# A fourth up-projection pair by seven half-size products, a last norm on two columns, transfers planned to land later, and modulations and low parts placed anew

## The chip, the cores and the metric

The kernel runs on one NeuronCore of a Trainium2 chip. Its engines work side by side, each through its own list of instructions in order: TensorE (PE in the profile; PEld is its loading of stationary operands), VectorE (DVE), ScalarE (ACT), GpSimd (POOL) and SyncE (SP, which here only issues transfers). They wait for each other by semaphores. The metric is the time of one execution on the device, in microseconds (us).

## What is computed

A trunk of two layers over 512 positions of width 1024 in float32. Layer 0 mixes tokens by retention, layer 1 by an mLSTM; each is followed by a feed-forward part with a causal convolution (3 taps). Every part starts from a normed and modulated copy of the residual stream and is added to it through a gate; shift, scale and gate come from a vector c.

```python
def rmsnorm(x, g):
    xf = x.astype(jnp.float32)
    xn = xf * lax.rsqrt(jnp.mean(xf * xf, axis=-1, keepdims=True) + EPS)
    return xn.astype(x.dtype) * g

def conv_ffn(h, w_up, conv_w, conv_b, w_down):
    u = causal_dwconv(h @ w_up, conv_w, conv_b)
    a, b = jnp.split(u, 2, axis=-1)
    return (jax.nn.silu(a) * b) @ w_down

def reference(x, c, ...):
    c_act = jax.nn.silu(c)
    for i in range(DEPTH):                       # 2 layers
        mod = c_act @ ada_w[i] + ada_b[i]        # 6 * 1024 values
        sh_t, sc_t, gt_t, sh_f, sc_f, gt_f = jnp.split(mod, 6, axis=-1)
        h = rmsnorm(x, norm_tok_g[i]) * (1.0 + sc_t) + sh_t
        y = retention_mixer(h, ...) if i == 0 else mlstm_mixer(h, ...)
        x = x + gt_t * y
        h = rmsnorm(x, norm_ffn_g[i]) * (1.0 + sc_f) + sh_f
        x = x + gt_f * conv_ffn(h, ffn_w_up[i], ffn_conv_w[i], ffn_conv_b[i], ffn_w_down[i])
    return rmsnorm(x, final_g)
```

The feed-forward part has 2816 inner columns, so its up-projection has 22 pairs of 128-column tiles (a and b); tile f and tile f + 22 make pair f.

## The kernel before

**Layout.** Activations are held transposed: eight tiles `x[m]` of 128 channels by 512 positions. "Halves" are positions 0 to 255 (HA) and 256 to 511 (HB).

**Three products for one.** A float32 value v is split into a high part (rounded to TensorE's reduced float32 by a cast on ACT) and a low part, v minus high. A product is then three matmuls: high by high, high by low, low by high (`mm3`, and the loops in `product`). The names in the profile follow from that: `whi` and `wlo` for weights, `hh` and `hl` for the normed input h, `ggh` and `ggl` for the gated inner values, `t24`, `t3` for sums of parts of h.

**Low parts in two ways.** `low_part` subtracts on DVE. `low_part_added` writes the negated high part on ACT (`wlo<-whi`) and lets a transfer issued by POOL add the raw weights to it (the accumulating `wlo<-raw`, `wlo<-wa`, `wlo<-ws`, `wlo<-wt`). Which way each of some 345 low parts takes is a default of its place, turned round for the numbers in the list `SWAPPED`.

**Pairs by seven products.** A tile pair with the whole h can be computed as 2 by 2 blocks (two tiles, two halves of positions; the inner sum in two halves as well) by seven half-size products in place of eight (`Fold`, `folded`, with sums of weight blocks `ws`, `wt`, made on DVE, and sums of h, made once by `Sums`). In each layer's feed-forward part the pairs 0 and 1 are computed while the norm is finished (`pf`), pairs 2 and 3 directly, as 24 products of 512 columns a tile (`pp`, `proj_item`), and pairs 4 to 21 (`FOLD_FROM` = 4) as units of `folded`. A unit is 84 products of 256 columns into two PSUM banks (`p` in the profile; `fs` and `fq` are copies out of them that ACT makes, and which later products into the same place wait for). Beside a unit stand the preparation of the next unit's weights, the convolution and gating of the pair before (`cv`), and, where the inner values are there, two tiles of the down-projection (`po`, with weights `raw` loaded by `Beside` into two buffers that the modulations also use).

**Modulations.** The 96 groups of mod are each a load of 0.5 MB (`ada`) and one multiply-and-sum over 1025 columns on DVE (`gemv`). 16 belong to the start; the other 80 are dealt out to stages by the table `SIDES`.

**The order.** Nothing runs in the order of the code. All calls are recorded (`Plan.add`), and `Plan.order` and `Plan.run` play them through with assumed costs, choosing for every engine the call that is ready and due first; the instructions are then issued in that order. A transfer is assumed to take 2.45 us per MB (5.4 where it accumulates), and what uses it is taken to be ready a fixed time after that: 1.2 us, or 2.4 us for an accumulating one. The due time of a transfer is put ahead of its user's by its length and 3.0 or 4.5 us (`tail`). At run time the real waits are made by semaphores, so a wrong assumption costs waiting in line: an instruction that is ready stands behind one that isn't.

**The start.** `ret_start` norms x by column sums: squares as stationary operand against one column of 1/1024 (`pms<-ones_d,sq`, 128x1), a root and a reciprocal of 4 columns, and a product of each column, repeated, with the identity to spread it over the partitions (`pms<-eye,rc`). Then h is made in eight slices, and the products of slice k wait for `hh` of that slice.

**The end.** The last down-projection is done by halves (`boundary`). `End` norms each half: `SquareSum` adds squares on DVE and splits the sum into two parts, `root` multiplies with a 128x128 matrix of 1/1024 (a mean that stands on all partitions), takes the root on ACT and the reciprocal on DVE over 256 columns; `use` multiplies each tile with gain and reciprocal (`out`) and sends two tiles to HBM at a time.

## Time and profile before

| | before |
|---|---|
| median of 3 runs | 1483.68 us (1481.92 to 1483.88) |
| the profiled execution | 1483.41 us |
| its span, first to last instruction | 1481.6 us |
| mean granted TensorE clock | 0.997 |
| instructions | 27248 |
| HBM read, written | 195.23 MB, 2.12 MB |
| DMA queue q0, POOL's transfers | 116.54 MB, 42.2% of 16 engines' span |
| DMA queue q1, SP's transfers | 197.11 MB, 38.3% |

Times of instructions are microseconds from the span's start. In a timeline a row gives start, duration, engine, line, operation, output <- inputs, shape and count, and in brackets how long the engine stood idle before it and what ended that. All operations are issued through one helper, so every row has the same line (L383), and rows are told apart by the names of tiles. The view of waits has, for an engine, whom it waited for, the total, the number and the longest wait. The view of windows has the busy time of each engine in a stretch. The chain is the work that ended last, followed back through what released it.

### The profile page before, as it was taken

The page shows a single profiled execution, that of the slowest core. Times are in us where ns is not written, and L with a number is a line of the kernel's source. Part 1 is how long each engine was busy: PE and PEld are TensorE (multiplying, and loading weights), DVE is VectorE, ACT ScalarE, POOL GpSimd, SP SyncE. Part 2 cuts the span into 40 slices and gives each one's busy share as a digit, 9 for nine tenths or more (in the row PEclk, how much of TensorE's full clock was granted, in tenths as well). Part 3 has the DMA queues.
Part 4 walks back from the last instruction along what each step waited for, and adds up shares of the span by engine and source line. Part 5 has one row for each costly group of instructions (what it writes and reads, how often), then busy time and mean ns, then how long its engine had stood idle before and what let it go on. Part 6 is the DMA issues. An engine that isn't in the chain of part 4 may idle for free.

```text
span 1481.6 us, 27248 instructions
## 1 busy us (share of the span) xinstructions
PE 1461.3 (99%) x10468; PEld 1368.8 (92%) x10468; DVE 1268.1 (86%) x2136; ACT 1075.9 (73%) x1606; POOL 279.0 (19%) x313
## 2 busy tenths in 40 slices
PE   9999999999999999999999999999999999999997
PEld 6799999998999999999999998999889899999997
DVE  7999979777989889898897999999889887777786
ACT  5678768777577676676668986989856876767662
POOL 0334132322111111111001222132211111111100
PEclk9999999999999999999999999999999999999998
DMA  9868989888798899999457895888687887888751
GB/s 363 252 175 207 282 209 230 224 250 212 206 215 215 241 261 258 265 261 266 118 180 171 207 246 144 208 221 199 205 239 201 213 219 194 194 208 191 190 125 58
DMA packets 93268, 315.65 MB, mean 213 GB/s; under 512 B 12225, under 2 KB 14657, under 8 KB 93138
## 3 DMA queue, kind: packets, MB, share of 16 engines
q0 software_dynamic: 32112, 116.54, 42.2%
q1 hardware_dynamic: 60738, 197.11, 38.3%
q8 instruction: 82, 1.34, 0.4%
q10 hardware_dynamic: 288, 0.27, 0.1%
q14 instruction: 48, 0.39, 0.1%
HBM read 195.23 MB, written 2.12 MB: 133 GB/s over the span
## 4 chain that ended last, share of the span: by engine, by line
PE 86%; DMA 7%; DVE 3%; ACT 2%; issue 2%; POOL 0%; DVEq 0%; ACTq 0%; SPq 0%; POOLq 0%
PE p L383 36%; PE po L383 27%; PE pv L383 9%; PE pav L383 4%; PE pp L383 3%; PE pf L383 3%; DMA wlo<-raw 2%; PE psc L383 2%; DMA raw<-w_in 1%; DMA wb<-w_up 1%; DMA raw<-w_dn 1%; PE pst L383 1%; DMA wlo<-wa 1%; DMA raw<-w_up 1%; PE pms L383 1%
## 5 line engine op out<-in xcount | busy, mean ns | idle before, releaser
L383 PE MATMUL p<-hh,whi 128*128 128x256 f32 (+1 forms) x994 | 275.6, 278 | 1.9 <-DVE p L383 1.9
L383 PE MATMUL p<-hl,whi 128*128 128x256 f32 x992 | 275.1, 277 | 0.0
L383 PE MATMUL p<-hh,wlo 128*128 128x256 f32 x992 | 273.4, 277 | 0.0
L383 ACT ACTIVATE wlo<-whi 128x1024 fp32r<-128x1024 f32 x223 | 235.0, 1057 | 39.8 <-PE po L383 15.1
L383 PEld LDWEIGHTS p<-hh,whi 128*128 128x128 f32 x994 | 187.1, 188 | 2.8 <-DVE p L383 2.3
L383 PEld LDWEIGHTS p<-hl,whi 128*128 128x128 f32 x992 | 186.7, 188 | 0.4
L383 PEld LDWEIGHTS p<-hh,wlo 128*128 128x128 f32 x992 | 185.6, 188 | 0.0
L383 PE MATMUL p<-t24h,whi 128*128 128x256 f32 x744 | 165.0, 279 | 4.1 <-ACT fs L383 3.1
L383 PE MATMUL po<-ggl,whi 128*128 128x512 f32 (+1 forms) x448 | 153.3, 343 | 0.0
L383 PE MATMUL po<-ggh,wlo 128*128 128x512 f32 (+1 forms) x448 | 153.1, 343 | 0.0
L383 PE MATMUL po<-ggh,whi 128*128 128x512 f32 (+1 forms) x448 | 152.4, 343 | 0.0
L383 ACT CAST whi<-raw 128x1024 fp32r<-128x1024 f32 (+1 forms) x117 | 118.0, 1019 | 44.8 <-DMA raw<-w_s 10.5
L383 PE MATMUL p<-t24l,whi 128*128 128x256 f32 x496 | 137.5, 277 | 0.0
L383 DVE SCALAR_TENSOR_TENSOR x<-po,mod,x 128x512 f32<-128x512 f32 (+1 forms) x184 | 113.0, 628 | 23.2 <-PE po L383 22.7
L383 PEld LDWEIGHTS p<-t24h,whi 128*128 128x128 f32 x744 | 126.3, 188 | 6.9 <-ACT fs L383 3.9
L383 DVE SCALAR_TENSOR_TENSOR ada<-ada,c_ext 128x1025 f32<-128x1025 f32 x96 | 119.5, 1246 | 6.5 <-DMA ada<-ada 6.4
L383 POOL DMA_DIRECT2D wlo<-wa x62 | 53.8, 867 | 355.4 <-ACT wlo L383 223.4
L383 PE MATMUL po<-yh,whi 128*128 128x256 f32 (+1 forms) x354 | 116.0, 329 | 0.3 <-ACT o L383 0.3
L383 PE MATMUL po<-yl,whi 128*128 128x256 f32 (+1 forms) x352 | 115.7, 329 | 0.0
L383 PE MATMUL po<-yh,wlo 128*128 128x256 f32 (+1 forms) x352 | 115.6, 329 | 0.0
L383 DVE SCALAR_TENSOR_TENSOR cv<-p,vecs,cv 128x511 f32<-128x511 f32 (+1 forms) x144 | 106.4, 744 | 9.9 <-ACT cv L383 9.2
L383 ACT CAST whi<-ws 128x1024 fp32r<-128x1024 f32 x86 | 90.0, 1050 | 28.5 <-DVE ws L383 23.5
(287 smaller groups left out, 4422.0 us busy)
## 6 DMA issues: line engine op xcount, KB each, us to landing
ada<-ada SPq DMA_DIRECT2D x96, 512.5 KB, 7.4
wlo<-ws POOLq DMA_DIRECT2D x68, 512.0 KB, 6.9
wlo<-wa POOLq DMA_DIRECT2D x62, 512.0 KB, 6.3
wlo<-wt POOLq DMA_DIRECT2D x44, 512.0 KB, 6.9
wlo<-raw POOLq DMA_DIRECT2D x41, 512.0 KB, 8.4
wa<-w_up SPq DMA_DIRECT2D x36, 512.0 KB, 6.9
wb<-w_up SPq DMA_DIRECT2D x36, 512.0 KB, 6.2
raw<-w_o SPq DMA_DIRECT2D x32, 512.0 KB, 6.6
```

What stands on the lines that cost most here:

```text
L383: getattr(c.obj, c.name)(*[real(v) for v in c.a], **{key: real(v) for key, v in c.k.items()})
```

## The change

1. `FOLD_FROM` 4 becomes 3: pair 3 joins the units of `folded` in both layers, so there are 19 units, and pair 2 alone is computed directly. The first down-projections stay beside pair 5 (`LATER`), so two units, pairs 3 and 4, and not one stand ahead of them.
2. `End` norms the last half as the start does: column sums on two columns of 128 positions, root and reciprocal of a 128x2 tile, and spreading by the identity. The gains are multiplied into copies of x on ACT as the tiles come (`xg`), and the last multiplication runs over strips of three, three, one and one tiles, each with its own transfer.
3. The plan's assumptions: loads are ready 2.5 us after their length instead of 1.2, accumulating transfers 3.0 instead of 2.4; loads are due 4.0 us ahead of that length instead of 3.0.
4. `SIDES`, `SWAPPED`, `QLOW` and `ML_LAST` are other numbers: the 80 modulations and the ways of the low parts are dealt out anew (31 instead of 32 modulations beside layer 0's units; the attention of the mLSTM's last head one weight tile later). In all 18 accumulating transfers go and DVE subtracts 20 low parts more.

```diff
-SIDES = [("ret q1", 2), ("ret v1", 2), ("ret g1", 6), ("ret g2", 2), ("ret q3", 2), ("ret g3", 5), ("ret o2", 6), ("fold0", 32), ("end0", 2), ("ml v1", 4), ("ml g1", 1), ("ml q2", 1), ("ml g2", 2), ("ml g3", 2), ("ml o1", 1), ("ml o2", 6), ("up1", 4)]
+SIDES = [("ret q1", 2), ("ret v1", 2), ("ret g1", 8), ("ret v2", 2), ("ret g2", 2), ("ret q3", 2), ("ret g3", 5), ("ret o2", 5), ("fold0", 31), ("end0", 2), ("ml v1", 5), ("ml g1", 2), ("ml q2", 1), ("ml v3", 2), ("ml o1", 6), ("ml o2", 2), ("up1", 1)]
-SWAPPED = (64, 67, 75, 150, 153, 158, 188, 192, 200, 208, 209, 211, 222, 241, 287, 301, 313)
-FOLD_FROM = 4
+SWAPPED = (61, 63, 64, 67, 75, 82, 83, 131, 132, 146, 153, 158, 179, 185, 188, 189, 192, 195, 200, 208, 209, 211, 218, 222, 223, 241, 247, 251, 255, 258, 264, 268, 270, 276, 277, 284, 285, 292, 301, 302, 310, 314, 315)
+FOLD_FROM = 3
+LATER = 5
+LANDING = (2.5, 3.0)
+LEAD = (4.0, 4.5)
-ML_LAST = (0, 1, -1, 2)
+ML_LAST = (1, 2, -1, 2)
-QLOW = (1, 3)
+QLOW = (0, 2)
     def tail(self, c):
-        return c.lat if not c.dma else c.dma + (4.5 if "accum_op" in c.k else 3.0)
+        return c.lat if not c.dma else c.dma + LEAD["accum_op" in c.k]
...
-                c.end = dma_free + (2.4 if "accum_op" in c.k else 1.2)
+                c.end = dma_free + LANDING["accum_op" in c.k]
...
-            if m == KT - self.direct - 1:
+            if m == KT - self.direct - 1 and not self.bare:
                 self.parts = Pair("ss")
                 self.parts.split(self.acc[:, r], r)
...
     class End(Norm):
-        direct = (0, 2)
+        direct, bare = (0, 2), True
+        strips = ((0, 3), (3, 6), (6, 7), (7, 8))
...
+        def square(self, p, m):
+            super().square(p, m)
+            if p:
+                for k0, k1 in self.strips:
+                    if k0 <= m < k1:
+                        if m == k0:
+                            self.scaled[k0] = wide("xg")
+                        at = (m - k0) * 256
+                        A.activation(self.scaled[k0][:, at : at + 256], x[m][:, HB], AF.Copy, scale=self.gain(m))
+
+        def last_root(self):
+            if self.eye is None:
+                self.eye = slot("eye")
+                S.dma_start(self.eye[:, :P], ident)
+            s, ps, out_ps, rc = self.s[1], bank("pms"), bank("pst"), slot("rc")
+            for n, sq in enumerate([s.acc] + s.last):
+                for t in range(2):
+                    PE.matmul(ps[:, t : t + 1], sq[:, 256 + t * P : 384 + t * P], ones["d"][:, :1].bitcast(F32),
+                              start=n + t == 0, stop=True, skip_group_check=True)
+            reciprocal_root(rc, ps[:, :2], slice(0, 2), eps_t[:])
+            for t in range(2):
+                PE.matmul(out_ps[:, 256 + t * P : 384 + t * P], rc[:, t : t + 1].broadcast_to([P, P]),
+                          self.eye[:, :P], start=t == 0, stop=True, skip_group_check=True)
+            self.rs[1] = out_ps
+
+        def last_use(self, k0, k1):
+            n = k1 - k0
+            o, each = wide("out"), lambda t: t.rearrange("p (a t) -> p a t", a=n)
+            V.tensor_tensor(each(o[:, : n * 256]), each(self.scaled[k0][:, : n * 256]),
+                            self.rs[1][:, HB].rearrange("p (a t) -> p a t", a=1).broadcast_to([P, n, 256]), op=ALU.mult)
+            S.dma_start(out[k0:k1, :, HB].rearrange("m p t -> p m t"), each(o[:, : n * 256]))
...
         def rest(self):
-            item([], lambda w: self.root(1))
-            for k in range(0, KT, 2):
-                item([], lambda w, k=k: self.use(1, k, k + 2))
+            item([], lambda w: self.last_root())
+            for k0, k1 in self.strips:
+                item([], lambda w, k0=k0, k1=k1: self.last_use(k0, k1))
...
-            downs = [None] * (5 - FOLD_FROM) + [p for gi in range(len(GROUPS) - 1) for p in self.down(gi)]
+            downs = [None] * (LATER - FOLD_FROM) + [p for gi in range(len(GROUPS) - 1) for p in self.down(gi)]
...
-            self.up(2)
+            th = self.pair(2)
             early(1)
-            th = self.pair(3)
-            proj_item(w[3], self.h, th, True)
+            proj_item(w[2], self.h, th, True)
             early(len(steps))
-            proj_item(w[3 + FT], self.h, lambda ps: (self.start.sums.turn(), th(ps)), True)
+            proj_item(w[2 + FT], self.h, lambda ps: (self.start.sums.turn(), th(ps)), True)
```

What the plan makes of it shows in the order of instructions. Three places follow. On ACT, at the end of layer 0's units, before the change: `whi<-raw` is the cast of the last down-projection weights of 1024 columns, `whi<-ws` and `whi<-wb` are casts of a unit's weights, `fs` is the copy that PE waits for.

```order
L383 CAST ggh_8080<-cv_8001 128x512
L383 CAST whi_8088<-raw_8019 128x1024
L383 CAST whi_8101<-ws_8071 128x1024
L383 CAST whi_8114<-wb_7812 128x512
L383 ACTIVATE cv_8122<-p_1340_7929,vecs 128x512
L383 COPY fs_8130<-p_1365_8104 128x256
```

And the same place after it, on the same engine:

```order
L386 COPY fq_8097<-p_1349_7978 128x256
L386 ACTIVATE cv_8135<-p_1349_7978,vecs 128x512
L386 CAST whi_8146<-ws_8124 128x1024
L386 CAST whi_8158<-wb_7888 128x512
L386 CAST whi_8166<-raw_8101 128x1024
L386 COPY fs_8180<-p_1374_8150 128x256
```

The cast of the loaded weights stood ahead of two casts and the convolution's first step; now it stands behind them, next to the copy `fs`.

On ACT, at the kernel's start, before the change: the four `hh` are the fifth to the eighth slice of h, `whi<-raw` the casts of the last weights of the start's own products and of the first query and key tiles behind them.

```order
L383 ACTIVATE hh_425<-xr_416,mod_86 128x512
L383 CAST whi_430<-raw_356 128x1024
L383 ACTIVATE wlo_440<-whi_430 128x1024
L383 ACTIVATE hh_459<-xr_450,mod_86 128x512
L383 CAST whi_486<-raw_409 128x1024
L383 CAST whi_496<-raw_419 128x1024
L383 ACTIVATE hh_505<-xr_491,mod_86 128x512
L383 ACTIVATE wlo_513<-whi_486 128x1024
L383 ACTIVATE hh_532<-xr_525,mod_86 128x512
```

After it:

```order
L386 ACTIVATE hh_423<-xr_416,mod_86 128x512
L386 CAST whi_428<-raw_348 128x1024
L386 ACTIVATE wlo_442<-whi_428 128x1024
L386 CAST whi_452<-raw_382 128x1024
L386 ACTIVATE hh_461<-xr_454,mod_86 128x512
L386 ACTIVATE wlo_467<-whi_452 128x1024
L386 ACTIVATE hh_503<-xr_496,mod_86 128x512
L386 CAST whi_508<-raw_431 128x1024
L386 CAST whi_516<-raw_439 128x1024
L386 ACTIVATE wlo_526<-whi_508 128x1024
L386 ACTIVATE hh_534<-xr_524,mod_86 128x512
```

One cast has moved ahead of the sixth slice (the second `hh` row), and no cast of a load is left directly ahead of the seventh; two stand ahead of the eighth. The load of that first cast is now issued right behind one modulation row, where two more such rows and another load went first.

On PE, the last rows before the change: `po` is the last down-projection, `pms` the mean of squares.

```order
L383 MATMUL po_17642<-ggh_17333,wlo_17203 128x256
L383 MATMUL pms_17668<-ssh_17638,ones_d 128x256
L383 MATMUL pms_17668<-ssl_17650,ones_d 128x256
L383 MATMUL pms_17668<-sq_17653,ones_d 128x256
L383 MATMUL pms_17668<-sq_17673,ones_d 128x256
```

After it:

```order
L386 MATMUL po_17748<-ggh_17436,wlo_17365 128x256
L386 MATMUL pms_17772<-ones_d,ssq_17598 128x1 x2
L386 MATMUL pms_17772<-ones_d,sq_17757 128x1 x2
L386 MATMUL pms_17772<-ones_d,sq_17776 128x1 x2
L386 MATMUL pst_17787<-eye_17294,rc_17784 128x128 x2
```

Four products of 256 columns have become six of one column, with the sums as the stationary operand, and two of 128 columns that spread the result.

More of the change, by code (lines that the diff above doesn't have):

```diff
@@ L672, in trunk, with __init__ @@
     class SquareSum:
-        def __init__(self, r, direct):
-            self.r, self.acc, self.last, self.direct = r, slot("ssq"), [], direct
+        def __init__(self, r, direct, bare=False):
+            self.r, self.acc, self.last, self.direct, self.bare = r, slot("ssq"), [], direct, bare
         def add(self, m):
@@ L1081, in trunk @@
     class Norm:
-        direct = DIRECT
+        direct, bare, eye = DIRECT, False, None
         def __init__(self):
@@ L1090, in square @@
             if m == 0:
-                self.s[p] = SquareSum(r, self.direct[p])
+                self.s[p] = SquareSum(r, self.direct[p], self.bare and p)
             self.s[p].add(m)
@@ L1214, in trunk, with __init__ @@
     class End(Norm):
-        direct = (0, 2)
+        direct, bare = (0, 2), True
+        strips = ((0, 3), (3, 6), (6, 7), (7, 8))
+        def __init__(self):
+            super().__init__()
+            self.scaled = {}
         def gain(self, m):
             return col("final", m)
+        def square(self, p, m):
[27 more added lines that the diff above has]
+            S.dma_start(out[k0:k1, :, HB].rearrange("m p t -> p m t"), each(o[:, : n * 256]))
         def use(self, p, k0, k1):
```

## The prediction

> **What bounds the kernel now.** First the page, for the shares; then the chain of waits; then PE's own waits.
>
> ```profile
> PE 1461.3 (99%) x10468; PEld 1368.8 (92%) x10468; DVE 1268.1 (86%) x2136; ACT 1075.9 (73%) x1606; POOL 279.0 (19%) x313
> ```
>
> TensorE is busy for 99% of the span, so time comes out in two ways alone: fewer matrix products, or shorter stretches in which PE waits. The next rows are all the long waits that the view of waits has for PE (us in total, times, longest).
>
> ```profile
> PE p L383 <- ACT fs L383: 3.1, 4, 1.3
> PE p L383 <- DVE p L383: 2.9, 4, 1.3
> PE pst L383 <- ACT hh L383: 1.6, 2, 1.0
> ```
>
> Together 7.6 us; the rest of what the span has beyond PE's busy time lies at the start and behind the last product. What a product costs must not be read from its duration. Two rows of the groups by shape (busy us, mean ns of one), then two pieces of the chain (start, us, what, count):
>
> ```profile
> L383 PE MATMUL p<-hh,whi 128*128 128x256 f32 x992 | 275.5, 278 | 1.9 <-DVE p L383 1.9
> ...
> L383 PE MATMUL pp<-hh,whi 128*128 128x512 f32 x104 | 40.5, 389 | 0.0
> ```
> ```profile
> 66.21 21.76 PE pp L383 x96
> ...
> 485.33 8.17 PE p L383 x72
> ```
>
> The means, 278 and 389 ns, overlap their neighbours. In the chain 96 products of 512 columns take 21.76 us, 226.7 ns each, and 72 of 256 columns 8.17 us, 113.5 ns each. Half the width is half the price, with nothing fixed on top.
>
> **Part 1, the pair by seven products.** Per layer 48 products of 512 columns go and 84 of 256 come; in both layers 96 and 168. 96 x 226.7 ns is the 21.76 us of the row above; 168 x 113.5 ns is 19.07 us. **Minus 2.7 us.** Around it DVE gets the sums of the folded weights. What that meets is read from the windows (us, then PE, PEld, DVE, ACT, POOL busy, clock, DMA share, GB/s):
>
> ```profile
> 425.00:441.00 16.00, 16.00 (x73) 13.25 (x72) 9.66 (x16) 13.78 (x18) 3.45 (x4) 1.00 0.93 209
> 470.00:485.00 15.00, 15.00 (x110) 14.01 (x109) 13.26 (x23) 9.72 (x15) 1.72 (x2) 1.00 1.04 288
> 485.00:650.00 165.00, 165.00 (x1188) 154.13 (x1187) 146.77 (x252) 114.74 (x159) 24.19 (x28) 1.00 0.94 254
> 800.00:900.00 100.00, 98.82 (x780) 96.00 (x779) 93.18 (x152) 88.44 (x141) 24.28 (x30) 1.00 0.88 224
> ```
> ```profile
> 485.37 0.75 DVE L383 SCALAR_TENSOR_TENSOR x<-po,mod,x 128x512 f32<-128x512 f32 x1
> ```
>
> A unit of the fold with down-projections (470 to 485) has 13.26 us of DVE work beside 15 us of PE. The change gives each layer one more unit without them: without two residual adds of 0.75 us DVE keeps 11.8 us, PE only 84 x 113.5 ns = 9.5 us. DVE is 2.3 us short in that unit, at most 4.6 us in the two layers. I cost it at nothing: just ahead of it, from 425 to 441, DVE is idle for 6.3 of 16 us, and in the long run of units (485 to 650) PE still never waits. Once that idle time is spent, the 2.3 us per layer show.
>
> **Part 2, the last half norm.** The end before, by engine: DVE, ACT, PE, and the chain's last piece of products.
>
> ```profile
> 1470.78 0.49 DVE L383 SCALAR_TENSOR_TENSOR x<-po,mod,x 128x256 f32<-128x256 f32 x1 [0.91 <-PE po L383]
> 1473.01 1.75 DVE L383 RECIPROCAL rs<-rs 128x256 f32<-128x256 f32 x1 [1.75 <-ACT rs L383]
> 1474.80 3.26 DVE L383 SCALAR_TENSOR_TENSOR out<-x,vecs,rs 128x256 f32<-128x256 f32 x8
> ```
> ```profile
> 1471.30 0.42 ACT L383 ACTIVATE sq<-x 128x256 f32<-128x256 f32 x1 [1.71 <-DVE x L383]
> 1472.51 0.47 ACT L383 ACTIVATE rs<-pms,eps_t 128x256 f32<-128x256 f32 x1 [0.79 <-PE pms L383]
> ```
> ```profile
> 1471.77 0.70 PE L383 MATMUL pms<-sq,ones_d 128*128 128x256 f32 x2 [0.35 <-ACT sq L383]
> ```
> ```profile
> 1458.02 12.74 PE po L383 x108
> ```
>
> Residual, square, mean, root, reciprocal, eight multiplications; DVE ends at 1478.06. The same form of sum on columns, root, reciprocal and spreading by the identity stands at this kernel's start; the last row is the nearest to a wide multiplication.
>
> ```profile
> 13.10 3.57 PE pms L383 x16
> 17.31 2.09 PE pms L383 x8
> ```
> ```profile
> 16.78 0.27 ACT L383 ACTIVATE rc<-pms,eps_t 128x4 f32<-128x4 f32 x1 [0.85 <-PE pms L383]
> ```
> ```profile
> 17.08 0.18 DVE L383 RECIPROCAL rc<-rc 128x4 f32<-128x4 f32 x1 [2.03 <-ACT rc L383]
> ```
> ```profile
> 1431.69 0.95 DVE L383 TENSOR_TENSOR wlo<-raw,whi 128x768 fp32r<-128x768 f32 x1
> ```
>
> Sixteen records for eight one-column sums: 0.223 us a record, two records a sum. The change has six sums after PE's last product, 12 records, 2.68 us from 1470.76, to 1473.44 (the last square is ready at 1471.72 and finds four sums still running). Root 0.27 and reciprocal 0.18, each with 0.04 to start: 1473.97. Two spreading products, half of the eight records in 2.09 us: 1475.02, and 0.05 to start. Then two multiplications of 768 columns at 0.95 and two of 256 at 0.41 (3.26 over eight): 2.72, to 1477.8. **Minus 0.3 us.** Bounds: minus 1.1, if four of the sums vanish under the residual and square, and plus 0.5, if the last transfers wait for each other. The eight scaled copies on ACT cost nothing: ACT stands idle 1.71 us before each square, and the last copy (0.42, after the square) ends before PE is done.
>
> The Trainium skill, "TensorE: Matmul & The Clock Gate", section Back-to-back issue gap, gives about 60 cycles (25 ns) to products of 1 to 64 columns. By it the twelve records would take 0.3 us as an estimate and the sum of all parts would come out some 1.5 us lower. This trace has 223 ns a record, nine times that, so the measurement decides.
>
> **Part 3, transfers planned to land later.** No instruction is added; the plan assumes that loads land 1.3 us later (accumulating ones 0.6), and puts other work ahead of what uses them. In the old plan a 512 KB load on a free queue lands 0.4 + 1.2 + 1.33 + 1.2 = 4.1 us after its issue starts, in the new one at 5.4. The trace:
>
> ```profile
> raw<-w_dn SPq DMA_DIRECT2D x32, 512.0 KB, 7.6
> ```
>
> So the old plan was too early, the new one less so. Two of PE's waits come from that. At the end of layer 0's fold:
>
> ```profile
> PE p L383 <- ACT fs L383: 1.3, 1, 1.3
> ```
> ```profile
> 681.41 0.60 ACT L383 CAST ggh<-cv 128x512 fp32r<-128x512 f32 x1
> 685.41 1.05 ACT L383 CAST whi<-raw 128x1024 fp32r<-128x1024 f32 x1 [3.39 <-DMA raw<-w_dn]
> 686.37 1.05 ACT L383 CAST whi<-ws 128x1024 fp32r<-128x1024 f32 x1
> 687.32 0.61 ACT L383 CAST whi<-wb 128x512 fp32r<-128x512 f32 x1
> 687.83 0.78 ACT L383 ACTIVATE cv<-p,vecs 128x512 f32<-128x512 f32 x1
> 688.50 0.36 ACT L383 COPY fs<-p 128x256 f32<-128x256 f32 x1
> ```
>
> ACT stands 3.39 us at a cast whose load is late; behind it queue two casts, a convolution and the copy fs that PE needs. In the new order those three come first and the cast stands directly ahead of fs (the order's rows, above): with the load at the same moment fs starts some 2.1 us earlier (688.50 less 686.37), more than PE's 1.3 us. **Minus 1.3.** At the start:
>
> ```profile
> PE pst L383 <- ACT hh L383: 1.0, 1, 1.0
> ```
> ```profile
> 53.27 1.05 ACT L383 CAST whi<-raw 128x1024 fp32r<-128x1024 f32 x1 [1.42 <-DMA raw<-w_in]
> 54.23 0.72 ACT L383 ACTIVATE hh<-xr,mod 128x512 fp32r<-128x512 f32 x1
> ```
> ```profile
> ada<-ada SPq DMA_DIRECT2D x1, 512.5 KB, 7.6
> ```
>
> The seventh slice of h stands behind that cast. In the new order one load goes out right after the modulation row issued at 35.58 (the last row above, landed 7.6 us later, at 43.2); its cast moves ahead of the sixth slice. An estimate: 0.5 MB more at about 340 GB/s is 1.5 us, so it lands at 44.7, and cast and slice end near 46.5; PE wants the sixth slice 24 x 226.7 ns = 5.4 us before its wait at 53.65, at 48.2. Nothing new is late, and PE's 1.0 us goes. **Minus 1.0.** For the other 5.3 of the 7.6 us I take no change: their places are reordered too, and the rows say neither way. Bounds for this part: minus 7.6, if all go, and plus 2.3, if two waits as long as these two come new.
>
> **Part 4, modulations and low parts placed anew.** 80 gemvs stay 80. 18 accumulating transfers go; DVE has 20 low parts more, ACT 18 negations fewer.
>
> ```profile
> 873.75 1.22 DVE L383 TENSOR_TENSOR wlo<-ws,whi 128x1024 fp32r<-128x1024 f32 x1
> ```
>
> 20 x 1.22 is 24 us of DVE over 1480, about five a stage. In the stage with least room (800 to 900) DVE is busy 93.18 of 100 us: 6.8 us of room against 4 x 1.22 = 4.9. Cost nothing, up to 4.9 us without that room.
>
> **The sum**, made against the profiled execution's own 1483.41 us (span 1481.6 and 1.8 around it; the median of the runs, 1483.68, is 0.02% above): 1483.4 - 2.7 - 0.3 - 1.3 - 1.0 = **1478.1 us**.
>
> **Rivals.**
> - The waits only move: landings change in the plan, but loads still go out when a buffer comes free, and the two late heads turn up elsewhere. For it: DMA share 0.93 to 1.04 in the windows. Against: the casts have demonstrably changed places with fs. Time: 1483.4 - 3.0 = 1480.4, on either side of it by one wait.
> - More waits go: the remaining 5.3 us as well, since the plan is nearer to the landings everywhere. For it: the other eight are waits for ACT or DVE too. Against: no row above shows a late load ahead of them. Time: 1478.1 - 5.3 = 1472.8.
> - DVE becomes the bound (the slower side). Place: the unit without down-projections in both layers, and the mLSTM's stage around 800 to 900. Price 4.6 + 4.9, and the two late heads stay: 1483.4 - 3.0 + 9.5 = 1489.9. It decides once DVE's idle time ahead of the unit falls under 2.3 us, or the room in the stage under 4.9; with about half of it the time is unchanged. For it: 93%. Against: 6.3 us idle before the fold.
> - Narrow products pay a fixed cost: if 278 and 389 ns were prices, a pair would cost 84 x 0.278 - 48 x 0.389 = 4.7 us more, and the sum would be 1483.4 + 9.4 - 2.6 = 1490.2. The pieces of the chain (113.5 against 226.7 ns) leave it next to nothing. The Trainium skill, "Perfetto Trace Analysis", section Matmuls, does say that larger matmuls are more efficient where possible; in this trace 256 columns are as efficient as 512.
>
> **Chances.** Forecast 0.48; waits only move 0.28 (0.10 of it faster, 0.18 the same); more waits go 0.08; DVE 0.15 (0.11 slower, 0.04 the same); fixed cost 0.01, slower. Faster by over 0.2% 0.66, within 0.2% 0.22, slower by over 0.2% 0.12; 0.2% (3 us) is about what a measurement of this kernel can tell from no change. The forecast's own range is 1475.5 to 1480.4. The range for 8 in 10 goes from 1474.0, most of the way to where all waits go, to 1486.5, about half way into DVE's case.
>
> **What would show it.** 1: the groups have 72 pp products of each kind instead of 104, and x84 pieces where x72 stood in the extra unit. 2: PE's one-column records end near 1473.4 less what was saved ahead, the reciprocal is under 0.2 us, DVE ends 2.7 us behind the spreading. 3: no row of PE waiting for fs near the fold's end or for hh near 53 us. 4: DVE's share about 88%. Wrong if PE waits for DVE p or fs in the fold's first units, or if the waits' sum stays above 6 us.

## The result, and the profile after

| | before | after |
|---|---|---|
| median | 1482.80 us (1480.26 to 1484.13, 21 runs) | 1485.12 us (1483.02 to 1489.25, 21 runs) |
| ratio to before, 95% interval | | 1.0017 [1.0011, 1.0024] |
| the profiled execution | 1483.41 us | 1483.02 us |
| its span | 1481.6 us | 1481.2 us |

The changed kernel is 2.3 us slower, within the 0.2% that the prediction called no change, and not 5.3 us faster as forecast. The two profiled executions hide this: that of before lies 0.6 us above its median, that of after is the shortest of its 21. What the trace shows of after is its best case. The experiments below hold a second execution of each order: up to the tail, run alone2 issues the instructions of before and run undo2 those of after.

First the answers to the rows shown of before: from the page, and from the groups by shape.

```profile
PE 1460.8 (99%) x10550; PEld 1372.3 (93%) x10550; DVE 1292.4 (87%) x2167; ACT 1064.9 (72%) x1604; POOL 267.1 (18%) x295
```
```profile
L386 PE MATMUL pp<-hh,whi 128*128 128x512 f32 x72 | 28.0, 390 | 0.0
```

72 direct products of each kind instead of 104, and a DVE share of 87%: the change did what it said. The view of waits for PE (us in total, times, longest):

```profile
PE p L386 <- DVE p L386: 4.8, 6, 1.6
...
PE pv L386 <- ACT fs L386: 1.4, 1, 1.4
PE pst L386 <- ACT hh L386: 1.3, 1, 1.3
...
PE p L386 <- ACT fs L386: 1.1, 1, 1.1
```

Together 8.6 us, where there were 7.6 before; the one for `hh` is now the first slice of h at 20 us, not the seventh at 53. The prediction said that more than 6 us would prove it wrong. (The sum moves between executions: in alone2, with the order of before, the same three rows give 5.4 us.) To see where the time went, PE's timeline is read at places that both programs have: the first product behind the start (`pp`), of layer 0's feed-forward part (`pf`), of layer 1's values (`pv`), of layer 1's feed-forward part, and the last of the down-projection. Before, then after:

```profile
66.05 0.39 PE L383 MATMUL pp<-hh,whi 128*128 128x512 f32 x1
...
402.14 0.28 PE L383 MATMUL pf<-hh,whi 128*128 128x256 f32 x1
...
771.19 0.39 PE L383 MATMUL pv<-whi,hh 128*128 128x512 f32 x1
...
1131.29 0.28 PE L383 MATMUL pf<-hh,whi 128*128 128x256 f32 x1
...
1470.46 0.28 PE L383 MATMUL po<-ggh,wlo 128*128 128x256 f32 x1
```
```profile
66.38 0.39 PE L386 MATMUL pp<-hh,whi 128*128 128x512 f32 x1
...
406.32 0.28 PE L386 MATMUL pf<-hh,whi 128*128 128x256 f32 x1
...
775.43 0.39 PE L386 MATMUL pv<-whi,hh 128*128 128x512 f32 x1
...
1133.91 0.28 PE L386 MATMUL pf<-hh,whi 128*128 128x256 f32 x1
...
1471.65 0.28 PE L386 MATMUL po<-ggh,wlo 128*128 128x256 f32 x1
```

| stage | before | after | change |
|---|---|---|---|
| start | 66.05 | 66.38 | +0.33 |
| retention | 336.09 | 339.94 | +3.85 |
| layer 0's feed-forward part | 369.05 | 369.11 | +0.06 |
| mLSTM | 360.10 | 358.48 | -1.62 |
| layer 1's feed-forward part | 339.17 | 337.74 | -1.43 |
| tail, to the end of the span | 11.14 | 9.55 | -1.59 |

Half of the 2.7 us of products shows in full, in layer 1 (-1.43). The half of layer 0 is gone, the tail gives five times what was forecast, and retention, where PE has the same products as before, takes 3.9 us more. In the mLSTM three waits of before, at 802, 878 and 1047 us (0.8, 0.7 and 1.5 us), are gone; the longest one there is now 0.45.

The second executions, alone2 and undo2, say which of these changes are firm. From alone2 to undo2 retention takes 3.9 us more as well (336.98 and 340.86), the mLSTM 2.2 less (360.62 and 358.45), layer 1's feed-forward part 1.6 less (338.90 and 337.30). But layer 0's feed-forward part takes 367.41 and 371.63, which is 4.2 us more, where the table has 0.06: from execution to execution of one order it moves by 1.6 to 2.5 us. The table's best case of after therefore hides a loss there.

What PE loses at one place is given below from start to start of two products, less the 113.5 or 226.7 ns that the first one takes; the view of waits counts 0.1 to 0.3 us less.

**Retention.** DVE, then POOL, at the longest new wait, PE's 1.77 us from 214.19 on:

```profile
211.85 3.82 DVE L386 TENSOR_TENSOR wlo<-wv,whi 128x1024 fp32r<-128x1024 f32 x1 [0.77 <-ACT whi L386]
215.60 0.42 DVE L386 TENSOR_TENSOR p<-p,fs 128x256 f32<-128x256 f32 x1
```
```profile
210.79 1.62 POOL L386 TENSOR_TENSOR rp<-rp,rp 128x512 f32<-128x512 f32 x1
212.04 1.21 POOL L386 DMA_DIRECT2D wlo<-ws  x1
212.66 1.92 POOL L386 TENSOR_TENSOR rp<-rp,rp 128x512 f32<-128x512 f32 x1
```

The low part `wlo` takes 1.21 us elsewhere and 3.82 here: 2.61 more. The two additions of POOL beside it cover 0.56 and 1.92 us of the row, 2.48 together. The short sum `p` that PE waits for stands behind it, though its other input was there at 212.1 (`fs`, 211.71 and 0.37 us on ACT). At 122 us PE waits 1.57 us for a copy `fs` in the same way. A sum on DVE took 4.19 us beside two additions of POOL, ACT stood 3.90 us for it, and caught up with its casts ahead of `fs`. The row of DVE, then ACT's:

```profile
111.62 4.19 DVE L386 TENSOR_TENSOR ws<-ws,wv 128x1024 f32<-128x1024 f32 x1
```
```profile
115.85 1.06 ACT L386 CAST whi<-ws 128x1024 fp32r<-128x1024 f32 x1 [3.90 <-DVE ws L386]
...
120.32 1.04 ACT L386 CAST whi<-ws 128x1024 fp32r<-128x1024 f32 x1
121.26 0.61 ACT L386 CAST qkh<-rp 128x512 fp32r<-128x512 f32 x1
121.78 1.05 ACT L386 ACTIVATE wlo<-whi 128x1024 fp32r<-128x1024 f32 x1
122.74 0.56 ACT L386 COPY z<-pav 128x512 f32<-128x512 f32 x1
123.20 0.37 ACT L386 COPY fs<-pv 128x256 f32<-128x256 f32 x1
```

Such long rows are in both traces: those over 0.15 us above the median of their tiles and shape exceed it by 26.5 us in all before and 24.6 after. What differs is who stands behind them. The Trainium skill, "SBUF — State Buffer", section SBUF: two separate sides, says that VectorE and GpSimd share a pair of ports which one of them, the one that starts first, holds for a whole instruction while the other is blocked. The 2.48 and 2.61 us agree with the blocking. Who comes first does not agree: the row of 4.19 us began at 111.62 and POOL's two additions at 111.87 by the profile, and still DVE's row is the long one (spans on POOL are rough).

**The folds' first units.** DVE, then ACT, at layer 0's first wait (444.17, 1.35 us): the sum `p` stands behind two steps of a convolution.

```profile
443.71 1.53 DVE L386 SCALAR_TENSOR_TENSOR cv<-pf,vecs,cv 128x511 f32<-128x511 f32 x2
445.16 0.42 DVE L386 TENSOR_TENSOR p<-p,fs 128x256 f32<-128x256 f32 x1
```
```profile
444.59 0.37 ACT L386 COPY fs<-p 128x256 f32<-128x256 f32 x1
```

The convolution holds the sum up by 0.2 us only, since its input `fs` ends at 444.96. The other 1.15 us are the way from PE's product over the copy and the sum back to PE. At layer 1's wait (1171.77, 1.22 us) the sum does stand in line, behind two sums of weights (0.68 us each).

**The tail**, on PE, then the chain's pieces for root, reciprocal, spreading and the first strip:

```profile
1471.77 0.50 PE L386 MATMUL pms<-ones_d,ssq 128*128 128x1 f32 x4
1472.14 0.58 PE L386 MATMUL pms<-ones_d,sq 128*128 128x1 f32 x4
1472.96 0.61 PE L386 MATMUL pms<-ones_d,sq 128*128 128x1 f32 x4 [0.24 <-ACT sq L386]
```
```profile
1473.61 0.27 ACT rc L386
...
1473.90 0.18 DVE rc L386
...
1474.12 0.72 PE pst L386 x4
...
1474.87 0.95 DVE out L386
```

Four one-column records take 0.37 us up to the next row (inside a row they start 0.11 us apart), and not 0.223 each, which the prediction took from the kernel's start. So the sums have caught up and wait 0.24 us for the last square.

### The profile page after: what moved, and what is told of

Same layout as the page of the kernel before. It is cut to its first block, busy times and chain, and to the rows that moved or that the text cites. A ratio compares the mean times of both kernels' runs of the same rounds, so it can differ in the third digit from the quotient of the medians.

```text
span 1481.2 us, 27389 instructions
## 1 busy us (share of the span) xinstructions
PE 1460.8 (99%) x10550; PEld 1372.3 (93%) x10550; DVE 1292.4 (87%) x2167; ACT 1064.9 (72%) x1604; POOL 267.1 (18%) x295
## 5 line engine op out<-in xcount | busy, mean ns | idle before, releaser
L386 PE MATMUL p<-hh,whi 128*128 128x256 f32 x1026 | 284.3, 278 | 2.5 <-DVE p L386 2.5
L386 PE MATMUL p<-hl,whi 128*128 128x256 f32 x1024 | 283.5, 277 | 0.0
L386 PE MATMUL p<-hh,wlo 128*128 128x256 f32 x1024 | 281.2, 277 | 0.0
L386 ACT ACTIVATE wlo<-whi 128x1024 fp32r<-128x1024 f32 (+1 forms) x205 | 215.4, 1055 | 26.3 <-PE po L386 15.6
L386 PEld LDWEIGHTS p<-hh,whi 128*128 128x128 f32 x1026 | 193.0, 188 | 3.7 <-DVE p L386 3.1
L386 PEld LDWEIGHTS p<-hl,whi 128*128 128x128 f32 x1024 | 192.8, 188 | 0.5
L386 PEld LDWEIGHTS p<-hh,wlo 128*128 128x128 f32 x1024 | 191.3, 188 | 0.0
L386 PE MATMUL p<-t24h,whi 128*128 128x256 f32 x768 | 170.1, 278 | 3.3 <-DVE p L386 2.2
L386 DVE SCALAR_TENSOR_TENSOR x<-po,mod,x 128x512 f32<-128x512 f32 (+1 forms) x184 | 113.5, 628 | 30.6 <-PE po L386 29.8
L386 DVE SCALAR_TENSOR_TENSOR cv<-p,vecs,cv 128x511 f32<-128x511 f32 (+1 forms) x152 | 111.2, 743 | 12.5 <-ACT cv L386 12.2
L386 POOL DMA_DIRECT2D wlo<-wa x55 | 47.6, 866 | 353.6 <-ACT wlo L386 168.7
```

What stands on the lines that cost most here:

```text
L386: getattr(c.obj, c.name)(*[real(v) for v in c.a], **{key: real(v) for key, v in c.k.items()})
```

## The experiments

Theories. **A**: each part saves what it should, and new waits take it back. **B**: what is missing is room on DVE (and on the queues), so whatever is late is late again. **C**: it is the order; PE's short operations stand in line behind work that could wait, and lists such as `SWAPPED` fit the one order for which they were made. Three more are set against C on the way: **D**, the new waits belong to the parts one by one; **E**, 2.5 us is a bad value for the landing; **L**, late loads. Each ratio below is to the kernel before as it ran beside that run (medians 1482.58 to 1483.07 us). The changed kernel did not run again; comparisons with its 1485.12 go across sessions, so its ratio of 1.0017 [1.0011, 1.0024] is the one to compare with.

| run | median us | ratio to before, 95% |
|---|---|---|
| alone1 | 1487.91 | 1.0035 [1.0022, 1.0048] |
| alone2 | 1481.37 | 0.9990 [0.9977, 1.0002] |
| alone3 | 1489.14 | 1.0043 [1.0030, 1.0056] |
| alone4 | 1489.26 | 1.0050 [1.0031, 1.0068] |
| undo1 | 1486.23 | 1.0021 [1.0012, 1.0030] |
| undo2 | 1485.98 | 1.0019 [1.0011, 1.0028] |
| undo3 | 1489.60 | 1.0043 [1.0027, 1.0059] |
| undo4 | 1492.73 | 1.0066 [1.0053, 1.0079] |
| jitter_b | 1488.69 | 1.0035 [1.0023, 1.0047] |
| jitter_a | 1491.21 | 1.0050 [1.0034, 1.0066] |
| moved | 1482.54 | 0.9994 [0.9983, 1.0004] |
| pool_adds | 1497.39 | 1.0094 [1.0079, 1.0108] |
| moved2 | 1481.18 | 0.9987 [0.9976, 0.9998] |
| best_b | 1482.20 | 0.9994 [0.9985, 1.0002] |

### One part alone, on the kernel before

```diff
# alone1
-FOLD_FROM = 4
+FOLD_FROM = 3
+LATER = 5
...
# alone2: End, SquareSum and Norm as changed
# alone3: LANDING and LEAD as changed
# alone4: SIDES, SWAPPED, ML_LAST and QLOW as changed
```

> The kernel before with part 1 alone (pair 3 by seven half-size products in both layers). Theory A, the parts save what they should and new waits from the new order take it back: 2.7 us of products go, new waits of about 1.2 us stand in the first units of both folds (as at 444 and 1171 us in the changed kernel) in place of the 0.9 us that stand there before, so about 1 us faster than before. Theory B, DVE's added work is itself the cost: a unit without down-projections is 2.3 us short of DVE in each layer, waits of 4.6 us, so 2 us slower than before. The prediction on record: 2.7 us faster.

> The kernel before with part 2 alone (last half norm on two columns). Theory A: as in the trace of the changed kernel, where the span ends 9.55 us after the last down-projection product starts and not 11.1, 1.6 us faster than before. The prediction on record: 0.3 us faster. Theory B has nothing to say here.

> The kernel before with part 3 alone (transfers planned to land later). Theory A: the waits at 53 us (1.1) and 687 us (1.4) go, but the whole order is made anew, and new waits of the kind seen at 121 and 214 us of the changed kernel (4 us in retention) come in their place: 1 to 3 us slower than before. Theory B: no instruction is added, so the same as before. The prediction on record: 2.3 us faster.

> The kernel before with part 4 alone (modulations and low parts dealt out anew; the list of turned low parts counts through the program, and with pair 3 direct its entries behind layer 0's first units fall on other low parts than in the changed kernel). Theory A: no work is added on PE, waits move, between 1 us faster and 3 us slower, and where it is slower the waits stand in retention. Theory B: 20 more low parts on DVE cost up to 5 us where DVE has least room (800 to 960 us), about 3 us slower, with PE waiting for DVE there. The prediction on record: no change.

Part 2 alone gives 1.7 us less in the median, as A expected from the trace, though its interval just reaches 1. Each of the other parts alone makes the kernel 5 to 6 us slower, which is more than A, B or the prediction had, while all four together cost 2.3 us: the parts do not add up. Their traces show the waits in line. In alone1 DVE stands 5.42 us for a load, and PE loses 2.7 us behind it, in layer 0's first units (and as much again in layer 1's, at 1207 us, where ACT stands 5.75 us for a load):

```profile
491.98 0.69 DVE L384 TENSOR_TENSOR ws<-wb 128x512 f32<-128x512 f32 x1 [5.42 <-DMA wb<-w_up]
```

In alone4, DVE and then ACT: DVE waits for the load of a modulation; `qkl`, 1.49 us for two, stands behind it, `fs` waits for `qkl`, and PE 4.6 us for `fs`.

```profile
317.00 1.23 DVE L383 SCALAR_TENSOR_TENSOR ada<-ada,c_ext 128x1025 f32<-128x1025 f32 x1 [4.30 <-DMA ada<-ada]
...
319.82 1.49 DVE L383 TENSOR_TENSOR qkl<-rp,qkh 128x512 fp32r<-128x512 f32 x2
```
```profile
321.42 0.37 ACT L383 COPY fs<-p 128x256 f32<-128x256 f32 x1 [4.72 <-DVE qkl L383]
```

Behind this wait TensorE runs at half its clock for 5 us. The window of alone4 right after it (clock in the third column from the end):

```profile
322.00:327.00 5.00, 5.00 (x24) 5.00 (x25) 2.63 (x4) 3.85 (x5) 0.00 (x0) 0.50 1.02 386
```

Products of 256 columns start 0.21 us apart there, not 0.11, which costs 2.5 us more. Wait and slow stretch together are 7.3 us, where before loses 1.2 at the same place: that is about all that alone4 loses. The same happens in undo3 (4.3 us at 316 us, then 2.5), and after alone1's wait at 1207 us (2.7 us, then 1.7), but not after its wait of 2.7 us at 492. So one long wait of PE can be most of what a new order costs. B's place for part 4, 800 to 960 us, is not where alone4 loses its time.

### One part undone, on the changed kernel

```diff
# undo1
-FOLD_FROM = 3
-LATER = 5
+FOLD_FROM = 4
...
# undo2: End, SquareSum and Norm as before
# undo3
-LANDING = (2.5, 3.0)
-LEAD = (4.0, 4.5)
+LANDING = (1.2, 2.4)
+LEAD = (3.0, 4.5)
# undo4: SIDES, SWAPPED, ML_LAST and QLOW as before
```

> The changed kernel with part 1 undone (pair 3 computed directly again, tail, landings and tables as changed; the low parts behind layer 0's units are counted differently, so some entries of the list fall on others). Theory C, every part that makes the plan anew costs about 5 to 6 us by waits elsewhere, as parts 1, 3 and 4 did alone, and the parts fit each other in the changed kernel: slower than the changed kernel, by the 2.7 us of products and some waits, about 1488 us. Theory D, the waits belong to the parts one by one, and part 1's are those in the first units of the folds (444 and 1171 us, 2.6 us together): these go, the products' 2.7 us come back, and the time stays at about 1485.

> The changed kernel with part 2 undone (last half norm as before). Both theories: the tail's 1.6 us come back, 1486.7 us, since nothing ahead of the last products is ordered otherwise.

> The changed kernel with part 3 undone (landings 1.2 and 2.4 us, lead 3.0 as before). Theory D: the wait of 1.6 us at 122 us and the 0.4 us behind it, which the kernel with part 3 alone has too, belong to part 3 and go; about 1483 us. Theory C: tables and landings fit each other, new waits come elsewhere, 1487 to 1491 us.

> The changed kernel with part 4 undone (modulations and low parts dealt out as before). Theory B, 20 more low parts on DVE cost time: up to 3 us faster than the changed kernel, 1482 to 1485 us. Theory C: 1487 to 1491 us, with the longest waits where loads land late, since 18 more accumulating transfers share the queues.

Parts 3 and 4 are harmful alone, and yet without them the changed kernel is slower, by 4.5 and 7.6 us (medians; C had at most 6 for undo4). That is again what a new order costs, and no measure of what a part is worth. B's forecast for part 4, up to 3 us faster without it, fails; a small cost of its 20 low parts could still hide under the new order. D's wait at 122 us does go in undo3, and others take its place (4.3 us at 316 us is the longest), as C expected. undo1, at 1486.23, lies between what C (1488) and D (1485) said. undo2 loses 0.9 us in the median; its interval overlaps that of the changed kernel, so the tail's gain is shown by alone2 and the traces rather than by it.

Two more things follow. In undo1, the view of waits has no row at all from 440 to 505 us and from 1150 to 1225: the waits in the folds' first units are part 1's. Layer 0's feed-forward part, measured as above, takes 367.1 us in it against 369.1 in the changed kernel (371.6 in undo2), though it has 1.36 us more of products, and layer 1's takes 337.69 against 337.74: what the products save there goes into waits as well. What undo1 loses it loses in the mLSTM (364.0 us against 358.5), where part 1 changes no product. And undo2 runs the changed kernel's order up to the tail: a second execution of it. There PE waits 4.4 us in layer 0's first units (440 to 505 us), where the first execution had 1.8, because loads land later. The first of them shows in a cast on ACT, in undo2 and in the changed kernel:

```profile
462.80 1.05 ACT L386 CAST whi<-wa 128x1024 fp32r<-128x1024 f32 x1 [2.56 <-DMA wa<-w_up]
```
```profile
460.00 1.04 ACT L386 CAST whi<-wa 128x1024 fp32r<-128x1024 f32 x1
```

The first execution got the load in time (4.9 us after its issue), the second did not (9.2 us). A second load, for the cast of `raw` at 500 us, landed 9.6 us after its issue where the first execution had 8.4. That fits a median of the changed kernel above its trace, as far as two executions can tell.

### A tenth of a microsecond

```diff
# jitter_b, on the kernel before
-                c.end = dma_free + (2.4 if "accum_op" in c.k else 1.2)
+                c.end = dma_free + (2.4 if "accum_op" in c.k else 1.3)
# jitter_a, on the changed kernel
-LANDING = (2.5, 3.0)
+LANDING = (2.6, 3.0)
```

> The kernel before with one assumption of the plan changed by 0.1 us: loads are taken to land 1.3 us after their length, not 1.2 (the changed kernel has 2.5). Some 440 of DVE's 2041 instructions and 350 of ACT's 1591 come in another place. Theory C (the tables fit the one order they were made with, and any new order meets some waits): 3 to 6 us slower than before, as with the landing of 2.5 us alone. Theory E (the landing of 2.5 us is too late as a value, and that cost the 6 us of part 3 alone): a twelfth of the step, so within 1 us of before.

> The changed kernel with the landing of loads assumed at 2.6 us, not 2.5. Theory C: 2 to 6 us slower than the changed kernel, 1487 to 1491 us. Theory E: within 1 us of it, 1484 to 1486 us.

Both are 6 us slower (1488.69 against 1482.58, 1491.21 against 1485.12). As a value, 2.5 us can hardly be worse than 1.2 when 1.3 costs the same 6 us: E falls. Of the eight runs whose order is made anew, for whatever reason, seven are 4.5 to 7.6 us slower than the kernel that they start from; undo1, at 1.1 us, is the exception. Why the two kernels' own orders are the good ones is argued and not shown: lists that fit one order, as C says, and an order that was merely picked out of many as the fastest would look the same, and no run fits the lists anew.

### The waits moved away by hand

```diff
-        for n in self.order():
+        for n in moved(self, self.order()):
...
+MOVED = ((869, 957), (943, 957), (695, 957), (895, 970), (882, 970), (698, 983), (856, 996),
+         (1869, 1821), (4122, 4254), (4121, 4254), (11914, 11809), (11805, 11809))
```

A pair (n, m) sets call n directly behind call m on its engine; all else keeps its order and its buffers, so nothing is planned anew.

> The changed kernel with twelve instructions set behind another one of their own engine, in five places, and nothing else: on ACT three ahead of the copy fs that PE waits for at 122 us and two ahead of the next one; on DVE two modulations behind the sums pv at 126 us, the low part of 3.82 us behind the sum p at 214 us, two steps of a convolution behind the sum p at 444 us, and two weight sums behind the sum p at 1171 us. Theory C (waits in line: PE's short operations stand behind long ones that could wait): the five waits, 1.57, 0.38, 1.77, 1.35 and 1.22 us, go and little comes instead: about 6 us faster than the changed kernel, 1478 to 1480 us, faster than before. Theory B (DVE has no room there, so whatever is put back is late next): most of it returns within the next units, 1483 us or more.

2.6 us come back, and 6 had been expected. Its trace has 0.42 us of the 1.57 at 122 us and nothing of the waits at 126 and 214: C holds in retention (337.5 us instead of 339.9). In layer 0's first units PE still waits, at 446, 464, 472 and 496 us, 5 us in all. That looks like B, but the moves did not bring the last three: undo2, in which nothing was moved, has them at the same products (467, 475 and 500 us) and as long (3.9 us in all in either run). Of the wait at 444 us only the 0.2 us behind the convolution could go; 1.2 us stay. The rest of that question is moved2's.

### POOL's additions against DVE

```diff
             getattr(c.obj, c.name)(...)
+            if n in EXTRA:
+                c.obj.tensor_tensor(self.spare[:], self.spare[:], self.spare[:], op=ALU.add)
```

> The changed kernel with 28 additions of 128x512 on POOL more, on a tile that nothing else uses, one behind each of POOL's transfers beside layer 0's units from 500 to 690 us; the order is otherwise the same. If DVE stands still while POOL adds (as the rows suggest in which DVE took 3.82 us for 1.21 beside two such additions): each takes up to 1.3 us from DVE, which has 20 us of room in these 190, some 25 us in all, so PE waits 5 us or more in this stretch, and rows of DVE there show up to 1.3 us above their usual length. If DVE and POOL run beside each other and the long rows had another cause: no change, 1484 to 1486 us.

12 us more, and DVE's rows exceed the median of their tiles and shape by 51.9 us in all, not 24.6: the 28 additions took 27.3, near the 25 that were forecast. Windows (us, then PE, PEld, DVE, ACT, POOL busy) of the changed kernel and of pool_adds:

```profile
500.00:690.00 190.00, 189.71 (x1352) 176.32 (x1351) 169.66 (x286) 128.13 (x178) 24.19 (x28) 1.00 0.91 247
```
```profile
500.00:690.00 190.00, 182.97 (x1279) 168.31 (x1280) 182.07 (x265) 121.68 (x170) 53.85 (x54) 0.99 0.86 232
```

DVE does 21 instructions fewer in the same 190 us and is busy 12.4 us longer, while ACT's mean row stays at 0.72 us. That DVE stands still beside POOL's additions is shown; and the stretch loses 6.7 us of PE although DVE still has 8 us idle: the blocked rows need not fill DVE to hold PE up.

### The rest, and the old order mended

```diff
# moved2: moved, and
+         (4453, 4451), (4642, 4470), (4706, 4642), (4643, 4706),
# best_b: alone2, and
+MOVED = ((411, 305), (412, 308), (6614, 6661), (6616, 6633), (6615, 6633), (8009, 7840), (8010, 7840),
+         (8495, 8755), (8612, 8754), (10383, 10541), (10493, 10541), (10668, 10541))
```

> The kernel with five places moved (1482.5 us), and two more beside layer 0's first units: on SP the load of down-projection weights (raw, used 18 us later) goes out behind the two loads of the unit's own weights, not ahead of them; on DVE a modulation, whose buffer the next raw load waits for, comes 2.4 us earlier, ahead of two steps of a convolution. Theory L (the waits at 464 and 496 us, 1.3 and 2.0 us, come from loads that go out late behind a full queue or a held buffer): both shrink by 1 us or more, about 1480 us. Theory B (in the units without down-projections something is always late, since nothing lies beside the chain of copy and sum): they move on to the next instruction, 1482 to 1483 us. The wait of 1.2 us at 446 us stays in both: there PE waits for its own last sum by way of the copy fq and the sum p, with no other product to do.

> The kernel before with part 2 alone (1481.4 us) and eleven instructions set behind another one of their own engine, in five places: the cast at 54 us behind the slice hh, the cast of late raw weights at 685 us behind two casts and a convolution step, two weight sums behind the sum p at 801 us, a modulation and an exponential behind fs and p at 877 us, and a low part and two sums behind the sum p at 1045 us. Theory C (waits in line): 0.8, 0.3 to 1.4, 0.9, 0.7 and 1.3 us go, 4 to 5 us in all, 1477 to 1478 us: faster than both kernels by over 0.2%. Theory B: less than half of it, 1479.5 us or more.

moved2 is faster than both kernels, by 1.8 us against before; its interval ends just below 1 (0.9998). In its profiled execution, the third fastest of 12, the waits at 464 and 496 us are gone, as theory L had it: they were late loads, one behind a load that was needed 18 us later, one for a buffer that a modulation held. That they are gone would prove little alone, since the first execution of the changed kernel did not have them either. But the load of `raw` was as slow as in moved (9.7 us from issue to landing against 10.1) and still landed at 491.57, ahead of its cast at 491.69, because it went out sooner. The 1.2 us at 446 us stay. PE's last product ahead of it, the copy `fq` (ACT), the sum (DVE) and PE again:

```profile
445.47 0.28 PE L386 MATMUL p<-hh,whi 128*128 128x256 f32 x1
446.75 0.38 PE L386 MATMUL p<-t24h,whi 128*128 128x256 f32 x1 [1.00 <-DVE p L386]
```
```profile
445.86 0.36 ACT L386 COPY fq<-p 128x256 f32<-128x256 f32 x1
```
```profile
446.27 0.42 DVE L386 TENSOR_TENSOR p<-p,fq 128x256 f32<-128x256 f32 x1
```

With down-projections in the unit there is a piece like this one of the changed kernel's chain to put between; a unit without them has nothing:

```profile
1223.94 2.75 PE po L386 x12
```

That is what part 1 pays in layer 0 for its 1.36 us.

best_b (twelve moves, where its expectation counts eleven) is a miss: 1482.20, no better than alone2. Its profiled execution reaches the last down-projection product 3.0 us sooner than before (1467.5 against 1470.5), and four of the five waits are gone or smaller, but the one at 877 us grew from 0.7 to 1.6 us: the exponential that was set behind one `fs` now brings its table load (1.28 us) ahead of the next. This execution is the fastest of its 12 (1479.0 to 1484.4), and one of the five waits was no lasting one: at 687 us alone2, with the order of before, loses 0.3 us and not 1.4. Which waits make the median was not seen.

## Why the prediction was wrong

- **Part 1, products: right** (-2.7; -1.43 in layer 1, and the piece of 84 products is there, at 1426.33). **Its cover: wrong.** "I cost it at nothing" took DVE's 6.3 us of idle time ahead of the unit for the cover. DVE still had 4.0 us of it (12.05 busy of the same 16 us in the changed kernel), but the unit has no products to lay beside the chain of copy and sum (1.2 us) and the loads behind it came late (1.3 and 2.0 us more in some executions). The rival named the place and the sign (PE waits for DVE `p` in the fold's first units), with want of DVE as the cause, which was at most a part of it. Against before, layer 1 took 1.4 us less, and layer 0 none less in the one pair of executions and 4.2 more in the other. Against undo1, which has the other new parts without this one, layer 1 gained 0.4 us at most and layer 0 nothing.
- **Part 2: the mechanism right, the size off** by the term of the sums: 12 records at 0.223 us, where they took 0.11. The 0.223 came from a row of the start in which TensorE ran slow (last section). From the last down-projection product to the end of the sums 1.9 us passed, not 3.0, and the spreading took 0.7, not 1.05. Measured -1.6, beyond the bound of -1.1. The reciprocal (0.18 against 0.18) and DVE's end behind the spreading (2.5 against 2.7) were as forecast. The 25 ns that the prediction took from the Trainium skill, "TensorE: Matmul & The Clock Gate", section Back-to-back issue gap, would have been too little by four times; the section itself calls its table the gap of an isolated product, without the loading of the stationary operand, and here every record loads its own.
- **Part 3: the step that failed.** The two waits that it was to remove did go: no wait for `hh` near 53 us, none for `fs` near 687. The second was partly luck, since alone2, with the order of before, has only 0.3 of its 1.4 us. But "for the other 5.3 of the 7.6 us I take no change" treated a plan that is made anew as if it stayed where no row was looked at. Waits went there too (three in the mLSTM), and longer ones came: 3.9 us in retention. The bound "plus 2.3, if two waits as long as these two come new" was the right thought at half its size or less: part 3 alone made the kernel 6.1 us slower, 5.0 of it in retention (341.09 us against 336.09). That an assumption nearer to the real landings gives a better order does not hold here with the lists kept: alone3 and jitter_b are both nearer, and both 6 us slower. The term for a new order was missing from parts 1 and 4 as well.
- **Part 4, no change: cannot be told from the rest.** Alone it makes the kernel 6 us slower, and undoing it does so by 7.6, both with a new order. Of its 24 us on DVE nothing is seen where DVE has least room: PE waits 0.3 us from 800 to 900 us.
- **The rivals.** "The waits only move" was the nearest: they did, and more came than went. It was priced with the two waits staying and nothing more, where a new order costs more. The measured 1485.12 lies inside the range for 8 in 10 (1474.0 to 1486.5), but that end of the range stood for a want of DVE, which is not what happened.

## What to carry to other kernels

A change to anything that a planner reads (an assumption, a table, a unit more) is a new order, and what was good about the old one can be lost: price that loss first, by a run with a change that means nothing, before pricing the parts. A unit whose filler work is taken away can pay for its chain from PE back to PE (1.2 us here), however idle the other engines are on average. Moving a single instruction behind the one that TensorE waits for, without planning anew, tells a wait in line from a want of room. But look at a second execution of the same order first: some waits come and go by themselves.

## What was not expected of the hardware

TensorE runs at half speed in one of two stretches of the start, or in both, and which it is does not hang on the program. Before, sixteen one-column records took 3.57 us (shown above) and the first slices from 20 us on ran at full speed; after, the same records took

```profile
13.09 1.95 PE L386 MATMUL pms<-ones_d,sq 128*128 128x1 f32 x16 [1.43 <-DVE sq L386]
```

and the products from 20 to 25 us took 0.43 us each for 0.23, 2.5 us in all, where the other stretch costs 1.6 (3.57 less 1.95). alone2, whose program is that of before up to the tail, is slow in both: 3.57 us for the sixteen records, and 0.43 us a product from 20 to 24 us. The granted clock shows it in some executions only. Windows of after, then of before and moved2 (the clock is the third column from the end):

```profile
15.00:25.00 10.00, 7.69 (x22) 5.86 (x22) 8.78 (x17) 5.01 (x8) 0.00 (x0) 0.52 1.02 417
```
```profile
20.00:25.00 5.00, 4.50 (x20) 3.71 (x21) 4.89 (x9) 2.38 (x4) 0.00 (x0) 1.00 1.02 416
```
```profile
20.00:25.00 5.00, 4.51 (x13) 3.57 (x14) 4.90 (x9) 2.35 (x4) 0.00 (x0) 1.00 1.02 416
```

moved2 has 13 products where before had 20, at a recorded clock of 1.00 in both: a row's length at the start is no price for the same row elsewhere, and the clock column does not always say so. The Trainium skill, "TensorE: Matmul & The Clock Gate", section Seeing it yourself, warns that the gate's events have been seen to be unreliable; these windows agree.
